# A decoder step on one core: two recurrences' small matrix products gathered into one group on the tensor engine

## The chip, the core and the metric

One core of one Trainium2 chip runs the whole step as one program. The metric is the device time of one launch in microseconds (us). Before the change it is 1133.66 us, the median of 3 runs (1133.45 to 1133.82).

## What is computed

One inference step of a hybrid decoder layer for 256 prompt tokens and 8 sample sequences of 8 tokens (320 tokens in all, model width 2048). One big projection of the normalised input feeds two recurrences; each is gated and projected, the two are merged by gates, and an output projection with a residual and a final norm ends the step. Cut to what matters here:

```python
h = rms_norm(x, norm_g)
p = jnp.einsum('nld,dp->nlp', h, w_in)            # 2048 -> 11,392 columns
# branch A (RWKV-7), 16 heads of 64, per token:
#   S_t = S_{t-1} diag(w_t) - (S_{t-1} kk_t)(kk_t * a_t)^T + v_t k_t^T ;  y_t = S_t r_t
y_a, s_a_new = rwkv7_recurrence(r_h, heads_a(decay), k_h, v_h, kk, heads_a(a), s_a)
# branch B (HGRN2), 8 heads, state 128 x 128, chunk by chunk:
#   S_t = diag(g_t) S_{t-1} + k_t v_t^T ;  o_t = S_t^T q_t
o_b, s_b_new = gla_chunkwise(heads_b(q_b), heads_b(k_b), heads_b(i_b), heads_b(log_g), s_b)
merged = sigmoid(p[gate_a]) * (y_a @ proj_a) + sigmoid(p[gate_b]) * (y_b @ proj_b)
y = x + merged @ w_out
```

All of it is float32; a large product is made of three passes in a rounded format (high*high, high*low, low*high), a small one is a plain float32 product, which the chip runs as two instructions.

## The kernel before

The program has three stages. A start normalises and transposes the input into two SBUF tiles, `hhi` and `hlo`. The **recurrence stage**, from about 30 to 696 us, is `record_all` (L1382): it goes over eight pairs `p` of A's heads, each with one head of B. For a pair it projects eight blocks of 128 columns (r, k, v, za for A; q, f, i, zb for B), each 16 x 3 products of 128x128 weights with 128x320 tokens into a PSUM tile named `mps`. I call these the *stream*: 3264 products, at L1441 in the profile. Then it computes `rwkv` (L780) and `hgrn` (L1163) for the pair. The last stage (from L1443 on) does the remaining gate columns, `proj_a`, `proj_b` and `w_out`; the change does not touch it.

In the recurrence stage nothing is issued as it is written. Every call goes to a `Recorder` (L69), which keeps a cost in ns for each operation, finds who depends on whom (`link`, L155) and then writes out an order for all engines together (`order`, L209). Each engine runs its own list in that order, so all its instructions stand at one line, L1441, the line that issues them. On the tensor engine the planner puts a small product into the list where it expects its operands to be there, 250 ns later than it computes (`MARGIN`), and fills the rest with stream products. So small products stand in the stream as *visits*: some stream products, one or more small ones, stream products again. The list is in order: if a small product's operand is late, the stream behind it waits too.

The tensor engine can also be cut into smaller tiles, for example four of 128 rows by 32 columns, whose products overlap. Products that are meant to run so are recorded as a *group* by `side_by_side` (L1360). The planner schedules the members of a group as if they all depended on whatever any of them depends on, and it accounts for each change of tile form. For B's operations it sets a wait of 6000 ns (`book.wait`, L1426 to L1428), by which B's group may be held back until another divided group opens the way.

The parts that the change touches, for one pair:

- *Pair products* of A (L895 to L907): for four chunks of 64 tokens and two heads, 64-row products as a group of eight into two PSUM tiles; for the samples (chunk 4) one 128x128 by 128x256 product, which holds both heads because `arp` is zero outside a head's own rows. Each result is masked into `g2`.
- *The turn of N* (L909 to L924): five transposes of `g2[:, ci, 0]`, for four chunks and the samples, copied into `xt` (ring `uB`) and from there into `M` (ring `uE`). The inverse of a triangular matrix is then built up from it in five doubling steps.
- *The chunk recurrence* `chunks` (L1013): per chunk the right side `rt`, which is `g2[:, ci, 0]` times `uv` plus, from the second chunk on, `arp` times the state, both added up in one PSUM tile; then two more products in a chain.
- *The samples' right side* in `samples` (L1054): a group of 12 products in four 128x32 tiles, into a tile of the ring `a` (three PSUM tiles for all of A).
- *B's group* (L1261): 42 products in 128x32 tiles. Behind it comes a transpose of `es` (L1279) and, ahead of it, one of `v` (L1181), both written for half the columns (profile form `128*64`).
- *The samples' decay* (L1086): GpSimd builds a diagonal tile `fd` twice in one buffer; each is read by one product.

The ring `y` is one more PSUM tile, used once a pair by the output products `py` (L1113).

## Time and profile before

| what | value |
|---|---|
| median of 3 runs | 1133.66 us |
| the profiled execution | 1133.88 us, its span 1132.1 us |
| TensorE (PE) busy | 1110.7 us, 98% of the span |
| VectorE (DVE) busy | 754.8 us, 67% |
| ScalarE (ACT) busy | 691.3 us, 61% |
| GpSimd (POOL) busy | 193.9 us, 17% |
| chain that ended last, by engine | PE 89%, DMA 3%, DVE 3%, issue 3% |

The profile is of one execution; a row gives an engine, a source line, an operation, the tiles it writes and reads, and the shapes. In the recurrence stage the line is always L1441, so operations are told apart by tiles and shapes. A tensor-engine row `128*32` is an instruction that uses 128 rows and 32 columns of the engine. A plain float32 product counts as two instructions. Tile `a` is any tile of A's PSUM ring, `b` one of B's, `y` the output ring; `uv`, `g`, `arp`, `bk`, `s0t`, `az`, `st`, `qz`, `es`, `fd` are as in the code; `pp` and `uB` belong to the doubling steps. In the timeline, instructions that follow each other with the same text stand in one row with their count, the start of the first, and the time until the last one's end; a PE row's length is modelled, so starts are what is measured.

### The profile page before, as it was taken

The numbers are of one execution on the slowest core, as the hardware profiler recorded it, in microseconds if no ns is written. First come the engines' busy times: TensorE is split into PE (matmuls) and PEld (weight loads), VectorE is DVE, ScalarE is ACT, GpSimd is POOL, SyncE is SP. The second block draws the span as 40 slices with busy tenths as digits, with TensorE's granted clock in tenths as the row PEclk, the third lists the DMA queues.
The fourth block names the chain that finished last, engine by engine and source line by source line (L and its number), as shares of the span: only waits on it lengthen the run. The fifth ranks groups of instructions, "written<-read, shape, count | busy, mean of one in ns | idle before, by whom it ended". The sixth has DMA issues, their size and how long they took to land.

```text
span 1132.1 us, 23282 instructions
## 1 busy us (share of the span) xinstructions
PE 1110.7 (98%) x9048; PEld 1072.6 (95%) x9048; DVE 754.8 (67%) x1586; ACT 691.3 (61%) x1580; POOL 193.9 (17%) x411
## 2 busy tenths in 40 slices
PE   6999999999999999999999999999999999999997
PEld 5998999999999999999999999999999999988886
DVE  7777788787887887878888776444444444436632
ACT  6767768777778678678677677444444444435322
POOL 9631131222321402302312200000000000000000
PEclk9999999999999999999999999999999999999999
DMA  5733645435435435445445345555555555587512
GB/s 177 198 112 97 169 115 134 139 108 138 131 112 155 132 98 152 130 114 148 117 114 153 112 125 146 150 151 149 154 150 150 150 149 149 149 252 250 186 38 93
DMA packets 283106, 159.85 MB, mean 141 GB/s; under 512 B 22893, under 2 KB 273264, under 8 KB 282356
## 3 DMA queue, kind: packets, MB, share of 16 engines
q1 hardware_dynamic: 282996, 158.37, 49.1%
q8 instruction: 71, 1.16, 0.4%
q14 instruction: 39, 0.32, 0.1%
HBM read 148.53 MB, written 9.81 MB: 140 GB/s over the span
## 4 chain that ended last, share of the span: by engine, by line
PE 89%; DMA 3%; DVE 3%; issue 3%; ACT 1%; POOL 1%; ACTq 0%; SPq 0%; POOLq 0%; DVEq 0%
PE mps L1441 40%; PE a L1441 11%; PE mps L360 6%; PE mps L361 6%; PE mps L359 6%; PE b L1441 3%; DMA raw<-in_w_out_dram 2%; PE po L1526 2%; PE po L1524 2%; PE po L1525 2%; PE ppb L360 2%; PE ppa L361 2%; PE ppa L360 2%; PE ppa L359 2%; PE ppb L359 2%
## 5 line engine op out<-in xcount | busy, mean ns | idle before, releaser
L1441 PE MATMUL mps<-hhi,wlo 128*128 128x320 f32 x1088 | 344.7, 317 | 0.0
L1441 PE MATMUL mps<-hhi,whi 128*128 128x320 f32 x1088 | 344.6, 317 | 0.0
L1441 PE MATMUL mps<-hlo,whi 128*128 128x320 f32 x1088 | 344.1, 316 | 0.0
L1441 PEld LDWEIGHTS mps<-hlo,whi 128*128 128x128 f32 x1088 | 204.9, 188 | 2.2 <-issue 1.2
L1441 PEld LDWEIGHTS mps<-hhi,whi 128*128 128x128 f32 x1088 | 204.8, 188 | 1.9 <-issue 0.8
L1441 PEld LDWEIGHTS mps<-hhi,wlo 128*128 128x128 f32 x1088 | 204.8, 188 | 1.4 <-issue 0.4
L349 ACT CAST whi<-raw 128x1024 fp32r<-128x1024 f32 x88 | 92.5, 1051 | 162.7 <-PE mps L360 107.3
L350 DVE TENSOR_TENSOR wlo<-raw,whi 128x1024 fp32r<-128x1024 f32 x88 | 107.9, 1226 | 125.0 <-ACT whi L349 124.8
L1441 DVE TENSOR_TENSOR wlo<-raw,whi 128x1024 fp32r<-128x1024 f32 x134 | 166.8, 1244 | 26.3 <-ACT whi L1441 24.5
L1441 ACT CAST whi<-raw 128x1024 fp32r<-128x1024 f32 x134 | 140.3, 1047 | 67.1 <-PE mps L1441 64.2
L359 PE MATMUL mps<-hhi,whi 128*128 128x320 f32 x448 | 138.4, 309 | 0.0
L360 PE MATMUL mps<-hlo,whi 128*128 128x320 f32 x448 | 138.4, 309 | 0.0
L361 PE MATMUL mps<-hhi,wlo 128*128 128x320 f32 x448 | 138.4, 309 | 0.0
L359 PEld LDWEIGHTS mps<-hhi,whi 128*128 128x128 f32 x448 | 84.1, 188 | 0.0
L360 PEld LDWEIGHTS mps<-hlo,whi 128*128 128x128 f32 x448 | 84.1, 188 | 0.0
L361 PEld LDWEIGHTS mps<-hhi,wlo 128*128 128x128 f32 x448 | 84.1, 188 | 0.0
L1513 DVE TENSOR_TENSOR wlo<-raw,whi 128x1024 fp32r<-128x1024 f32 x32 | 38.5, 1223 | 39.2 <-ACT whi L1512 36.4
L1512 ACT CAST whi<-raw 128x1024 fp32r<-128x1024 f32 x32 | 32.9, 1050 | 49.0 <-DMA raw<-in_w_out_dram 24.1
L1524 PE MATMUL po<-whi,mhi 128*128 128x512 f32 x128 | 50.1, 391 | 0.7 <-DVE gbt L1481 0.7
L1526 PE MATMUL po<-wlo,mhi 128*128 128x512 f32 x128 | 50.1, 392 | 0.1
L1525 PE MATMUL po<-whi,mlo 128*128 128x512 f32 x128 | 50.0, 391 | 0.0
L359 PE MATMUL ppa<-yah,whi 128*128 128x320 f32 x128 | 39.6, 309 | 0.0
(423 smaller groups left out, 2224.1 us busy)
## 6 DMA issues: line engine op xcount, KB each, us to landing
raw<-in_w_in_dram SPq DMA_DIRECT2D x194, 512.0 KB
raw<-in_w_out_dram SPq DMA_DIRECT2D x32, 512.0 KB
raw<-in_proj_a_dram SPq DMA_DIRECT2D x16, 512.0 KB
raw<-in_proj_b_dram SPq DMA_DIRECT2D x16, 512.0 KB
s<-in_state_hgrn_dram SPq DMA_DIRECT2D x8, 512.0 KB
out_dram<-s SPq DMA_DIRECT2D x8, 512.0 KB
s<-in_state_rwkv_dram SPq DMA_DIRECT2D x8, 256.0 KB
out_dram<-s SPq DMA_DIRECT2D x8, 256.0 KB
```

Of the source, the lines that this page charges most:

```text
L349: S.copy(hi[:, ks], raw[:, ks])
L350: sub.tensor_sub(lo[:, ks], raw[:, ks], hi[:, ks].bitcast(F32))
L359: T.matmul(dst, hi[:, q, :], xhi[:, k, :], start=(k == 0), stop=False)
L360: T.matmul(dst, hi[:, q, :], xlo[:, k, :], start=False, stop=False)
L361: T.matmul(dst, lo[:, q, :], xhi[:, k, :], start=False, stop=(k == nk - 1))
L1441: o.fn(*o.args, **o.kw)
L1512: S.copy(hi, raw)
L1513: V.tensor_sub(lo, raw, hi.bitcast(F32))
L1524: T.matmul(pt, h, hi, start=first, stop=False)
L1525: T.matmul(pt, l, hi, start=False, stop=False)
L1526: T.matmul(pt, h, lo, start=False, stop=end)
```

## The change

It makes one group of three sets of products. `rwkv` and `hgrn` become generators that hand out their products at a `yield`; `record_all` records both lists as one group and then runs the rest of each. The group has the samples' 12 products, 16 new 128x32 products which compute what `uv` gives to the right sides of all four chunks (they go into the ring `y`, are copied once into `rv`, and are added to the state's part by VectorE), and B's 42. `book.wait` is no longer set. The samples' pair products are made by head, in the group of the other pair products, and masked by two operations. For the turn of N, ScalarE first gathers two chunks in one tile `nd` (ring `big`), so three transposes do and one copy takes them out. The two half-width transposes of B take a full 128 columns.

```diff
         banks = [aps("pg") for _ in HS]
-        side_by_side([((banks[h][:, 128 * ci:128 * ci + 128], bk2[HS[h], ci]..., arp[HS[h], ci, :, h]), ...) for ci in range(4) for h in range(2)])
+        own = [ring(psy, "y", [128, 512], 1, F32, None), aps("pg")]
+        side_by_side([((banks[h][:, 128 * ci:128 * ci + 128] if ci < 4 else own[h][:, :128],
+                        bk2[HS[h], ci]..., arp[HS[h], ci, :, h]), ...) for ci in range(5) for h in range(2)])
...
-        ps = aps("pg")
-        T.matmul(ps[:, :256], bk2[:, 4]..., arp[:, 4]..., start=True, stop=True)
-        V.tensor_mul(g2[:, 4], ps[:, :256]..., mk[:, 2, :, None]...)
+        for h in range(2):
+            V.tensor_mul(g2[:, 4, :, h], own[h][:, :128]..., mk[:, 2])
+        nd = at("nd", (128, 2, 2, 64), tag="big")
+        for c_ in range(2):
+            S.copy(nd[HS[c_]], g2[HS[c_], c_:4:2, 0])
         ps = aps("pM")
-        for ci in range(5):
-            turn(ps, ci, g2[:, ci, 0].rearrange("p h t -> p (h t)"))
+        for cp in range(2):
+            T.transpose(ps[:, 128 * cp:128 * cp + 128], nd[:, cp].rearrange("p h t -> p (h t)"), ident)
+        T.transpose(ps[:, 256:384], g2[:, 4, 0].rearrange("p h t -> p (h t)"), ident)
-        S.copy(xt[:, 0:4]..., half(ps, 2))
-        S.copy(xt[:, 4], ps[:, 384:448])
+        S.copy(xt[:, 0:5].rearrange("p c t -> p (c t)"), ps[:, :320])
...
+        pr = ring(psy, "y", [128, 512], 1, F32, None)
+        psr = aps("psr")
+        work = []                       # first the samples' 12 products, as before
+        for ci in range(4):
+            for h in range(2):
+                for a_ in range(2):
+                    o_ = 64 * h + 32 * a_
+                    work.append(((pr[o_:o_ + 32, 64 * ci:64 * ci + 64], g2[:, ci, 0, h, 32 * a_:32 * a_ + 32],
+                                  uv[:, ci, h]), dict(start=True, stop=True)))
+        yield work
         def chunks():
-                ps = aps("pr")
-                T.matmul(ps[:, :128], g2[:, ci, 0]..., uv[:, ci]..., start=True, stop=st_ is None)
-                if st_ is not None:
-                    T.matmul(ps[:, :128], arp[:, ci, 0]..., st_, start=False, stop=True)
-                V.tensor_copy(rt[tk, 0], ps[HS[0], 0:64])
-                S.copy(rt[tk, 1], ps[HS[1], 64:128])
+                if st_ is None:
+                    V.tensor_copy(rt[tk, 0], pr[HS[0], 0:64])
+                    S.copy(rt[tk, 1], pr[HS[1], 0:64])
+                    rv = at("rv", (128, 3, 64), tag="uK")
+                    S.copy(rv.rearrange("p c v -> p (c v)"), pr[:, 64:256])
+                else:
+                    ps = aps("pr")
+                    T.matmul(ps[:, :128], arp[:, ci, 0]..., st_, start=True, stop=True)
+                    for h in range(2):
+                        V.tensor_add(rt[tk, h], ps[HS[h], 64 * h:64 * h + 64], rv[HS[h], ci - 1])
...
-        T.transpose(ps[0:64, 256:384], v[:, NP_:], ident)
+        T.transpose(ps[:, 256:384], v[:, NT - 128:], ident)
...
-        side_by_side([(x_, dict(start=True, stop=True)) for x_ in work])
+        yield [(x_, dict(start=True, stop=True)) for x_ in work]
...
-        T.transpose(ps[0:64, :128], es[:, 1], ident)
+        T.transpose(ps[:, :128], es.rearrange("p x t -> p (x t)"), ident)
...
-            rwkv(p, *(io[key] for key in ("r", "k", "v", "za")))
-            book.wait = book.WAIT
-            hgrn(p, *(io[key] for key in ("q", "f", "i", "zb")))
-            book.wait = 0
+            both = rwkv(p, ...), hgrn(p, ...)
+            side_by_side(next(both[0]) + next(both[1]))
+            for gen in both:
+                run(gen)
```

The planner then writes another order. Three places of it, all of TensorE; a product counts once here, and `mps` rows are the stream.

The third pair, before: first the samples' group (`s0t,az` and `uv,g`, 12 products), then, 60 stream products on, B's group of 42.

```order
L1441 MATMUL mps<-hhi,whi 128x320
L1441 MATMUL a_488<-s0t_497,az_500 32x64 x8
L1441 MATMUL a_488<-uv_495,g_0_502 32x64 x4
L1441 MATMUL mps<-hlo,whi 128x320
L1441 MATMUL a_486<-rhs_507,yz 128x128
```

```order
L1441 MATMUL mps<-hhi,whi 128x320
L1441 MATMUL b_524<-s_0_520,qz 32x128 x8
L1441 MATMUL b_523<-w_0_529,w_0_521 32x32 x8
L1441 MATMUL b_523<-w_0_528 32x32 x8
L1441 MATMUL b_523<-o_531 32x32 x8
L1441 MATMUL b_523<-ket_532 32x32 x4
L1441 MATMUL b_523<-ks_534,s_0_533 32x64 x4
L1441 MATMUL b_523<-w_0_529,w_0_521 32x32 x2
L1441 MATMUL mps<-hlo,whi 128x320
L1441 MATMUL a_486<-st_514,arp 128x128
```

The same pair in the changed kernel: one group of 70, then one stream product, then four small products that hang on it.

```order
L1448 MATMUL mps<-hhi,wlo 128x320
L1448 MATMUL a_488<-s0t_497,az_500 32x64 x8
L1448 MATMUL a_488<-uv_495,g_0_502 32x64 x4
L1448 MATMUL y_503<-uv_495,g_0_502 32x64 x16
L1448 MATMUL b_513<-s_0_509,qz 32x128 x8
L1448 MATMUL b_512<-w_0_518,w_0_510 32x32 x8
L1448 MATMUL b_512<-w_0_517 32x32 x8
L1448 MATMUL b_512<-o_520 32x32 x8
L1448 MATMUL b_512<-ket_521 32x32 x4
L1448 MATMUL b_512<-ks_523,s_0_522 32x64 x4
L1448 MATMUL b_512<-w_0_518,w_0_510 32x32 x2
L1448 MATMUL mps<-hhi,whi 128x320
```

What moved: the two groups stand at one place, with the 16 new products between them; the third pair's group comes after 1140 stream products, where the two came after 1117 and 1177. Over the stage, 22 visits held 128x32 products and 16 do now (8 of these are the output products); small products stand in 387 visits both times.

The first pair, the second `fd` product, before:

```order
L1441 MATMUL a_486<-fd_511,jr_sum 128x256
L1441 MATMUL mps<-hlo,whi 128x320
L1441 MATMUL mps<-hhi,wlo 128x320
L1441 MATMUL mps<-hhi,whi 128x320
L1441 MATMUL mps<-hlo,whi 128x320
L1441 MATMUL a_487<-rhs_507,yz 128x128
L1441 MATMUL a_488<-rhs_0_508,ys_503 128x128
L1441 MATMUL a_486<-fd_511,jr_sum 128x256
```

and now, with the first `fd` product right behind the group:

```order
L1448 MATMUL a_488<-fd_530,jr_sum 128x256
L1448 MATMUL a_486<-rhs_526,yz 128x128
L1448 MATMUL a_487<-rhs_0_527,ys_505 128x128
L1448 MATMUL b_513<-ident,es_524 128x128
L1448 MATMUL mps<-hhi,whi 128x320
L1448 MATMUL mps<-hlo,whi 128x320
L1448 MATMUL mps<-hhi,wlo 128x320
L1448 MATMUL mps<-hhi,whi 128x320
L1448 MATMUL a_486<-uv_495,bk_506 128x128
L1448 MATMUL mps<-hlo,whi 128x320
L1448 MATMUL a_488<-fd_530,jr_sum 128x256
```

What moved: between the two `fd` products stand five stream products and four small ones, where there were four and two; and `fd` now comes behind B's group, for which VectorE has by then made all operands. The second `fd` product stood after 353 stream products in this pair; the new group stands after 368.

## Rows read from the trace of the kernel before

**Rows 1.** The page's part 1: engine, busy us (share of the span) x instructions.

```profile
PE 1110.7 (98%) x9048; PEld 1072.6 (95%) x9048; DVE 754.8 (67%) x1586; ACT 691.3 (61%) x1580; POOL 193.9 (17%) x411
```

**Rows 2.** Busy time of each engine in a stretch of the recurrence stage: the stretch, its us, then PE, PEld, DVE, ACT, POOL busy (x instructions), granted clock, DMA share, GB/s.

```profile
200.00:280.00 80.00, 80.00 (x804) 77.86 (x793) 65.14 (x159) 56.90 (x151) 20.74 (x44) 1.00 0.46 126
```

**Rows 3.** A group of PE instructions by line, tiles and shape: xcount | busy us, mean ns of one | idle before.

```profile
L1441 PE MATMUL a<-uv,g 128*128 128x128 f32 x64 | 12.4, 275 | 0.0
```

**Rows 4.** PE's timeline, first pair, two stream products with 23 more between them (start us, us, what).

```profile
59.74 0.31 PE L1441 MATMUL mps<-hhi,wlo 128*128 128x320 f32 x1
...
63.26 0.31 PE L1441 MATMUL mps<-hhi,wlo 128*128 128x320 f32 x1
```

**Rows 5.** The same timeline: a visit of two float32 128x128 products (four instructions), and one of the same with the chunk's `uv,g` product behind them; in each, one stream product that isn't shown stands ahead of the last row.

```profile
85.18 0.31 PE L1441 MATMUL mps<-hhi,wlo 128*128 128x320 f32 x1
85.33 0.60 PE L1441 MATMUL a<-pp,uB 128*128 128x128 f32 x4
...
85.92 0.31 PE L1441 MATMUL mps<-hlo,whi 128*128 128x320 f32 x1
...
90.25 0.31 PE L1441 MATMUL mps<-hhi,whi 128*128 128x320 f32 x1
90.40 0.60 PE L1441 MATMUL a<-pp,uB 128*128 128x128 f32 x4
90.84 0.39 PE L1441 MATMUL a<-uv,g 128*128 128x128 f32 x2
...
91.21 0.31 PE L1441 MATMUL mps<-hhi,wlo 128*128 128x320 f32 x1
```

**Rows 6.** PE's timeline, third pair: the samples' group alone.

```profile
253.83 0.31 PE L1441 MATMUL mps<-hhi,whi 128*128 128x320 f32 x1
254.06 0.43 PE L1441 MATMUL a<-s0t,az 128*32 128x64 f32 x16
254.31 0.29 PE L1441 MATMUL a<-uv,g 128*32 128x64 f32 x8
254.54 0.41 PE L1441 MATMUL mps<-hlo,whi 128*128 128x320 f32 x1
```

**Rows 7.** PE's timeline, third pair: B's group alone (its other products lie between the second row and the third), then a visit and the transpose of `es`; one stream product that isn't shown stands ahead of the last row.

```profile
267.31 0.31 PE L1441 MATMUL mps<-hhi,whi 128*128 128x320 f32 x1
267.55 0.64 PE L1441 MATMUL b<-s,qz 128*32 128x128 f32 x16
...
268.76 0.42 PE L1441 MATMUL mps<-hlo,whi 128*128 128x320 f32 x1
269.02 0.38 PE L1441 MATMUL a<-st,arp 128*128 128x128 f32 x2
269.16 0.40 PE L1441 MATMUL mps<-hhi,wlo 128*128 128x320 f32 x1
269.39 0.28 PE L1441 MATMUL b<-ident,es 128*64 128x128 f32 x1
...
269.66 0.31 PE L1441 MATMUL mps<-hlo,whi 128*128 128x320 f32 x1
```

**Rows 8.** PE's timeline, fourth pair: both groups in one visit.

```profile
338.28 0.31 PE L1441 MATMUL mps<-hhi,whi 128*128 128x320 f32 x1
338.52 0.43 PE L1441 MATMUL a<-s0t,az 128*32 128x64 f32 x16
...
338.88 0.62 PE L1441 MATMUL b<-s,qz 128*32 128x128 f32 x16
...
340.07 0.41 PE L1441 MATMUL mps<-hlo,whi 128*128 128x320 f32 x1
```

**Rows 9.** PE's timeline, third pair: the pair products' group, the samples' product behind it, and the turn's transposes.

```profile
226.25 1.16 PE L1441 MATMUL a<-arp,bk 64*128 64x128 f32 x16
227.34 0.41 PE L1441 MATMUL mps<-hhi,wlo 128*128 128x320 f32 x1
227.59 0.59 PE L1441 MATMUL a<-arp,bk 128*128 128x256 f32 x2
227.83 0.50 PE L1441 MATMUL mps<-hhi,whi 128*128 128x320 f32 x1
228.17 0.31 PE L1441 MATMUL mps<-hlo,whi 128*128 128x320 f32 x1
...
229.05 0.71 PE L1441 MATMUL a<-ident,g 128*128 128x128 f32 x5
```

**Rows 10.** The first pair around 95 us: PE's, POOL's and DVE's timelines (idle time before an instruction and who ended it in brackets), then the group of all `fd` operations: xcount, ns min/median/max, first and last start.

```profile
97.25 0.39 PE L1441 MATMUL a<-fd,jr_sum 128*128 128x256 f32 x1 [1.68 <-POOL fd L1441]
...
94.63 2.57 POOL L1441 TENSOR_TENSOR fd<-id,fq 128x256 fp32r<-128x256 f32 x1 [22.01 <-PE a L1441]
...
94.77 1.21 DVE L1441 TENSOR_TENSOR wlo<-raw,whi 128x1024 fp32r<-128x1024 f32 x1
...
96.51 0.21 DVE L1441 TENSOR_TENSOR qz<-es,q 128x64 f32<-128x64 f32 x1
...
L1441 POOL TENSOR_TENSOR fd<-id,fq x16: 607/616/2572, 51.7 to 660.3; 128x256 fp32r<-128x256 f32 x16
```

**Rows 11.** Groups of DVE instructions, as in rows 3.

```profile
L1441 DVE COPY rhs<-a 64x64 f32<-64x64 f32 x40 | 8.6, 215 | 8.5 <-PE a L1441 3.8 <-ACT rhs L1441 3.8
L1441 DVE TENSOR_TENSOR g<-a,mk 128x256 f32<-128x256 f32 x8 | 3.3, 417 | 0.0
```

More of the change, by code (lines that the diff above doesn't have):

```diff
@@ L895, in rwkv @@
         banks = [aps("pg") for _ in HS]
-        side_by_side([((banks[h][:, 128 * ci:128 * ci + 128], bk2[HS[h], ci].rearrange("p j t -> p (j t)"),
-                        arp[HS[h], ci, :, h]), dict(start=True, stop=True)) for ci in range(4) for h in range(2)])
+        own = [ring(psy, "y", [128, 512], 1, F32, None), aps("pg")]
+        side_by_side([((banks[h][:, 128 * ci:128 * ci + 128] if ci < 4 else own[h][:, :128],
+                        bk2[HS[h], ci].rearrange("p j t -> p (j t)"), arp[HS[h], ci, :, h]),
+                       dict(start=True, stop=True)) for ci in range(5) for h in range(2)])
         for h in range(2):
@@ L1011, in rwkv @@
         states = []
+        pr = ring(psy, "y", [128, 512], 1, F32, None)
+        psr = aps("psr")
+        work = []
+        for step in range(3):
+            for h in range(2):
+                for a_ in range(2):
+                    l_, r_ = (az[:, h, a_, 32 * step:32 * step + 32], s0t[:, 2 * a_ + step, 64 * h:64 * h + 64]) \
+                        if step < 2 else (g2[:, 4, 0, h, 32 * a_:32 * a_ + 32], uv[:, 4, h])
+                    o_ = 64 * h + 32 * a_
+                    work.append(((psr[o_:o_ + 32, :64], l_, r_), dict(start=step == 0, stop=step == 2)))
+        for ci in range(4):
+            for h in range(2):
+                for a_ in range(2):
+                    o_ = 64 * h + 32 * a_
+                    work.append(((pr[o_:o_ + 32, 64 * ci:64 * ci + 64], g2[:, ci, 0, h, 32 * a_:32 * a_ + 32],
+                                  uv[:, ci, h]), dict(start=True, stop=True)))
+        yield work
         def chunks():
@@ L1017, in chunks @@
                 tk = HS[c_]
[L1018 to L1021 removed]
                 rt = at("rhs", (128, 2, 64))
[L1023 to L1024 removed]
+                if st_ is None:
[5 more added lines that the diff above has]
+                    ps = aps("pr")
+                    T.matmul(ps[:, :128], arp[:, ci, 0].rearrange("p h t -> p (h t)"), st_, start=True, stop=True)
+                    for h in range(2):
+                        V.tensor_add(rt[tk, h], ps[HS[h], 64 * h:64 * h + 64], rv[HS[h], ci - 1])
                 yield
@@ L1054, in samples @@
         def samples():
-            ps = aps("psr")
-            work = []
-            for step in range(3):
-                for h in range(2):
-                    for a_ in range(2):
-                        l_, r_ = (az[:, h, a_, 32 * step:32 * step + 32], s0t[:, 2 * a_ + step, 64 * h:64 * h + 64]) \
-                            if step < 2 else (g2[:, 4, 0, h, 32 * a_:32 * a_ + 32], uv[:, 4, h])
-                        o_ = 64 * h + 32 * a_
-                        work.append(((ps[o_:o_ + 32, :64], l_, r_), dict(start=step == 0, stop=step == 2)))
-            side_by_side(work)
             rhs = at("rhs2", (128, 2, 64))
-            V.tensor_copy(rhs[0:64, 0], ps[HS[0], :64])
-            S.copy(rhs[0:64, 1], ps[HS[1], :64])
+            V.tensor_copy(rhs[0:64, 0], psr[HS[0], :64])
+            S.copy(rhs[0:64, 1], psr[HS[1], :64])
             yield
@@ L1283, in hgrn @@
             for j in (0, 2):
-                S.copy(k3[32 * j:32 * j + 32, g], ps[own, :128])
-            V.tensor_sub(k3[32:64, g], ps[own, :128], k3[0:32, g].bitcast(F32))
+                S.copy(k3[32 * j:32 * j + 32, g], ps[64 + 32 * g:96 + 32 * g, :128])
+            V.tensor_sub(k3[32:64, g], ps[64 + 32 * g:96 + 32 * g, :128], k3[0:32, g].bitcast(F32))
         ps = bps("pot")
```

15 lines of the change are left out of this document (3 added, 12 removed).

## The prediction

> **What bounds the kernel now.** I read the page's busy shares first, then the stretches, then TensorE's timeline. TensorE is busy for 98% of the span, VectorE for 67% [rows 1]. In a stretch of the recurrence stage TensorE is busy for all of 80.00 us at the full granted clock, VectorE for 65.14, ScalarE for 56.90 [rows 2]. So in this stage the time is the length of TensorE's list, and each thing has to be priced by what it takes out of that list, not by its own length: products overlap, and a row's 0.31 us of a stream product is not its share. The timeline gives the share. From the start of one stream product to that of the 24th behind it pass 63.26 - 59.74 = 3.52 us, 0.1467 us each [rows 4]. The price of a visit is then the time between the stream products around it, less 0.147 for each stream product in it.
>
> The cover that hides other engines is the stream itself: while a chain of small operations waits for VectorE or ScalarE, stream products run. It has 3264 products in both orders, and in both the last output products stand some 100 of them (15 us at 0.147) ahead of the stream's end, so the stage's end is not moved by a longer chain.
>
> **Part by part**, per pair of heads, then times eight.
>
> *Right sides' value part, out.* A visit with four instructions of 128x128 takes 85.92 - 85.18 - 2 x 0.147 = 0.45 us; with the chunk's `uv,g` product behind them 91.21 - 90.25 - 2 x 0.147 = 0.67 [rows 5]. So one such product (two instructions) costs 0.22 us. There are 64 instructions [rows 3], 32 products: **-7.0 us**.
>
> *The same part, in 128x32 tiles.* It is 16 products, 32 instructions of 128x32 with 64 columns, the very shape of the `s0t,az` and `uv,g` rows. In the fourth pair 24 of these start between 338.52 and 338.88 us, 0.015 us each [rows 8]; 32 take 0.48 us, **+3.8 us** in all. Bounds: B's 84 instructions take 268.76 - 267.55 = 1.21 us, 0.0144 each [rows 7], 3.7 us in all; the last eight of a group with the way out of it take 254.54 - 254.31 = 0.23, 0.029 each [rows 6], 7.4 in all. I take 0.015, since it is read inside such a group, where the new ones stand.
>
> The Trainium skill speaks against this price: the page "TensorE: Matmul & The Clock Gate", section "Wait — 56ns, not 53.3ns?", says that starts of small matmuls are never less than about 25 ns apart. By that the term would be 32 x 25 ns = 0.8 us a pair, 6.4 us in all. The trace disagrees, with 15 ns.
>
> *Samples' pair products.* The visit of the 128x256 product takes 228.17 - 227.34 = 0.83 us; without it the two steps would be 0.25 (what follows any group: 227.59 - 227.34) and 0.147, so 0.43 goes. Four instructions are added to a group in which 16 take 227.34 - 226.25 = 1.09 us, 0.068 each [rows 9]: +0.27. Together -0.16, **-1.3 us**.
>
> *Turn of N.* Five transposes take 0.71 us from the first start to the last end, and one lasts about 0.28 [rows 7, 9]: (0.71 - 0.28) / 4 = 0.11 each. Two go: **-1.8 us**. The two copies into `nd` come before the transposes on the chain, but the stream covers a chain; ScalarE pays for them, beside the bound.
>
> *One group for two.* Alone, the samples' group takes 254.54 - 253.83 - 0.147 = 0.56 us [rows 6], B's 268.76 - 267.31 - 0.147 = 1.30 [rows 7]; both in one visit take 340.07 - 338.28 - 0.147 = 1.64 [rows 8]. That saves 0.22, and one slow step behind a group (269.02 - 268.76 = 0.26 in place of 0.147) [rows 7], 0.33 in all. In two pairs they already stood together, so six gain: -2.0. But in four of these six B's group had the samples' 64x64 group (`pds`) beside it, which now stands alone in all eight. That gives back between nothing and 4 x 0.33; I take the middle, +0.7. Net **-1.3 us**.
>
> *Half-width transposes.* The `es` visit takes 269.66 - 269.16 - 2 x 0.147 = 0.21 us [rows 7], a full-width transpose 0.11. If each of 16 lost that 0.10, it would be 1.6; the one of `v` I have no clean row for. Between 0 and -1.6 I take **-0.4 us**, since such a transpose is a change of tile form only where it stands alone.
>
> *Waits.* In the first pair TensorE stood still for 1.68 us for the second `fd`: GpSimd took 2.57 us for what takes 0.616 in the median, while VectorE ran operations with two SBUF operands, a 1.21 us weight subtraction among them [rows 10]. In the new order the two `fd` products are further apart, and VectorE's products for B are done ahead of the group. So I expect this wait to go: -1.7. New small ones will come, since four products stand one stream product behind the group and hang on copies out of it: I put +0.7. Net **-1.0 us**, between -1.7 and nothing.
>
> *Costs beside the bound.* VectorE gets six additions for three copies at 0.215 us, 0.65 us a pair, and one mask operation of 0.417 us becomes two, under 0.42 more [rows 11]. On 65.14 us in 80 [rows 2] that is 83% at most. What hides it is TensorE's list; if that cover were gone, it would be 8 x 1.07 = 8.6 us. No DMA is added or removed.
>
> The sum: -7.0 + 3.8 - 1.3 - 1.8 - 1.3 - 0.4 - 1.0 = -9.0 us. The profiled execution took 1133.88 us, 0.22 above the median, so the median goes from 1133.66 to **1124.7 us**.
>
> **Rivals.**
>
> *New waits eat half.* The visit behind the group needs `rt` and both halves of `rhs`, copied by VectorE and ScalarE out of a group that ends 0.147 us earlier. A copy is 0.215 us [rows 11], and a weight cast of ScalarE's can stand in front of it. At 0.5 us a pair this is +4: 1128.7 us. For it: the list is in order, and one late operand did hold it for 1.68 us [rows 10]. Against: the samples' and the values' products come first in the group, and B's 84 instructions, 1.2 us [rows 7], run behind them while the copies are made. Chance 0.14.
>
> *B's operands come late, and it gets slower.* The samples' side has to wait for B's last operand now, and a late one holds TensorE, stream included. In the first pair B's last operand, `qz`, was made at 96.51 us, behind a weight subtraction of 1.21 us [rows 10]. If every group waited as long as the `fd` of the first pair, 1.68 us, it would be 13.4 us on -8.0 (the sum without waits): 1139 us. It decides from 1.0 us a pair. Against: that was ahead of the second `fd` product at 97.25 us [rows 10], which stood after 353 stream products; the new group comes after 368, 2.2 us of stream later, and the planner adds 250 ns for every operand. Chance 0.04.
>
> *Starts 25 ns apart.* If the new products did not run as closely as those in the rows, but at 25 ns, the group would be 32 x 0.010 = 0.32 us a pair longer, +2.6: 1127.3 us. Rows 6 and 8 speak against it; for it only that the group gets longer, 140 instructions, than any in the rows. Chance 0.04. It is the rule of "TensorE: Matmul & The Clock Gate" cited above.
>
> *TensorE is not what is short.* If VectorE or ScalarE sets the pace somewhere in a pair, a shorter list makes TensorE wait for weights, and 1133 us stays. For it: VectorE is 81% busy and gets more. Against: TensorE is busy for 80.00 of 80.00 us [rows 2]. Chance 0.06. The Trainium skill warns of this in "TensorEngine Tiling (Array Packing)", section "PSUM Bottleneck": tiling makes TensorE faster but not the copies out of PSUM.
>
> **How the numbers follow.** The forecast has 0.72. A difference of 0.2%, 2.3 us, is about what a measurement of this kernel can tell from none. Forecast, eaten half and 25 ns are all faster by more: 0.72 + 0.14 + 0.04 = 0.90; within 0.2%: 0.06; slower: 0.04. The range: with the low ends (values' part -0.1, `pds` -0.7, half-width -1.2, waits -0.7) it is 2.7 below, 1122.0; with the high ends (+3.6, +0.6, +0.4, +1.0) 5.6 above, 1130.3, which takes in the first and third rival. The prices are read from starts given to 0.01 us, so I round outward below, and give 1121.5 to 1130.0.
>
> **What would show it.** Right: the group's visit with 140 instructions takes about 2.1 us (1.64 + 0.48); `uv,g` in 128*128 form is gone, and its chunk visits hold a lone `st,arp`; the pair products' group takes 0.27 longer with no 128x256 visit behind it; TensorE's only long wait for POOL is gone; the last stage takes as long as before. Wrong: PE idle time in front of `rhs,yz` or of the group's first product, with ACT or DVE as releaser; a stream step above 0.147 away from visits; or a group longer than 2.5 us.

## The result and the profile of the changed kernel

The changed kernel takes 1124.47 us (median of 6 runs, 1123.9 to 1124.7); the kernel before, beside it on the same chip, 1133.74. The ratio is 0.9917, 95% interval 0.9904 to 0.9929. The forecast was 1124.7 with a range of 1121.5 to 1130.0. The profiled execution took 1124.7 us with a span of 1122.0.

Page, part 1, and the stretch from 200 to 280 us (length, then PE, PEld, DVE, ACT and POOL busy with counts, granted clock, DMA share, GB/s). They answer to [rows 1, 2]:

```profile
PE 1102.9 (98%) x9240; PEld 1066.5 (95%) x9240; DVE 760.4 (68%) x1618; ACT 693.2 (62%) x1572; POOL 192.8 (17%) x411
...
200.00:280.00 80.00, 79.66 (x792) 77.61 (x791) 66.30 (x165) 59.90 (x157) 18.27 (x42) 1.00 0.45 125
```

TensorE has 192 instructions more and is busy for 7.8 us less. It is still what is short, but not for the whole stretch: 0.34 us are idle in it now, and we come to them. VectorE and ScalarE do a little more beside the bound; VectorE 5.6 us in all, where 8.6 was priced.

TensorE's timeline in the third pair, from the last stream product ahead of the joint group to the end of the visit behind it (start, duration, line, output<-inputs, tile, shape, count). It answers to [rows 6 to 8]:

```profile
252.47 0.31 PE L1448 MATMUL mps<-hhi,wlo 128*128 128x320 f32 x1
252.71 0.43 PE L1448 MATMUL a<-s0t,az 128*32 128x64 f32 x16
252.95 0.29 PE L1448 MATMUL a<-uv,g 128*32 128x64 f32 x8
253.07 0.63 PE L1448 MATMUL y<-uv,g 128*32 128x64 f32 x32
253.51 0.62 PE L1448 MATMUL b<-s,qz 128*32 128x128 f32 x16
...
254.70 0.42 PE L1448 MATMUL mps<-hhi,whi 128*128 128x320 f32 x1
254.96 0.28 PE L1448 MATMUL a<-fd,jr_sum 128*128 128x256 f32 x1
255.08 0.38 PE L1448 MATMUL a<-rhs,yz 128*128 128x128 f32 x2
255.30 0.39 PE L1448 MATMUL a<-rhs,ys 128*128 128x128 f32 x2
255.52 0.27 PE L1448 MATMUL b<-ident,es 128*128 128x128 f32 x1
255.55 0.39 PE L1448 MATMUL mps<-hlo,whi 128*128 128x320 f32 x1
...
258.76 0.31 PE L1448 MATMUL mps<-hhi,wlo 128*128 128x320 f32 x1
259.00 0.66 PE L1448 MATMUL a<-big,rhs 64*64 64x256 f32 x8
259.60 0.41 PE L1448 MATMUL mps<-hhi,whi 128*128 128x320 f32 x1
```

Start the reading at the stream rows. The group of 140 instructions stands between 252.47 and 254.70: 2.23 us, less 0.147 for the stream product, 2.09 (2.088 before rounding). Its new piece, the 32 instructions `y<-uv,g`, runs from 253.07 to 253.51, 0.014 us each. Behind it the visit with `rhs` shows no idle time in brackets: the copies out of the group are in time. The group `a<-big,rhs` (`pds`) stands alone.

The pair products of the fourth pair, which answer to [rows 9] (there it is the third pair); the 128x256 visit behind them is gone:

```profile
301.25 1.16 PE L1448 MATMUL a<-arp,bk 64*128 64x128 f32 x16
...
302.57 0.42 PE L1448 MATMUL mps<-hlo,whi 128*128 128x320 f32 x1
302.82 0.31 PE L1448 MATMUL mps<-hhi,wlo 128*128 128x320 f32 x1
...
305.67 0.40 PE L1448 MATMUL mps<-hlo,whi 128*128 128x320 f32 x1
305.90 0.27 PE L1448 MATMUL a<-ident,bks 128*128 128x128 f32 x1
305.93 0.39 PE L1448 MATMUL mps<-hhi,wlo 128*128 128x320 f32 x1
306.16 0.31 PE L1448 MATMUL mps<-hhi,whi 128*128 128x320 f32 x1
```

The group takes 302.57 - 301.25 = 1.32 us from its first start, against 1.09 before: 0.23 for four instructions. The last four rows are a transpose of full width that stands alone: 306.16 - 305.67 - 2 x 0.147 = 0.20 us. We need it for the half-width ones.

TensorE's waits (operation, line, releaser, total us, times, longest) and GpSimd's `fd` (min/median/max ns), which answer to [rows 10]:

```profile
PE a L1448 <- DVE pp L1448: 0.7, 2, 0.3
...
L1448 POOL TENSOR_TENSOR fd<-id,fq x16: 607/614/1651, 51.0 to 648.2; 128x256 fp32r<-128x256 f32 x16
```

The 1.68 us for `fd` are gone, though one `fd` still takes 1.65 us instead of 0.61: nobody waits for it now. A new pair of waits stands there, for `pp`. One of the two, on three engines:

```profile
231.39 1.13 DVE L1448 TENSOR_TENSOR uB<-id,uB 128x160 f32<-128x160 f32 x1
232.44 0.48 DVE L1448 TENSOR_TENSOR pp<-a,lvz 128x320 f32<-128x320 f32 x1
...
231.30 1.04 POOL L1448 TENSOR_TENSOR big<-bk,seq 128x512 f32<-128x512 f32 x1
...
232.41 0.31 PE L1448 MATMUL mps<-hhi,wlo 128*128 128x320 f32 x1
233.07 0.85 PE L1448 MATMUL a<-pp,uB 128*128 128x128 f32 x6 [0.34 <-DVE pp L1448]
```

`uB` takes 1.13 us on VectorE while GpSimd works on `big`; `pp` stands behind it, and TensorE starts `pp,uB` 0.66 us behind the stream product before it. The bracket's 0.34 is only the time with nothing left in the engine: what a visit lost is the distance of the starts, 0.58 us by the visit's price.

### A price list to read the experiments by

To compare the kernels I fitted one price for each kind of instruction, visit and group to all visits of the kernel before, and applied these prices to the order of each other kernel (*list*, us over the recurrence stage, an estimate). *Visits* is what the trace has, that is, the time between stream products beyond 0.147 each. The last column is the part of the difference in visits over 0.12 us above their price, with their number. List and visits come from one execution of each kernel.

| kernel | median us | list | visits | over 0.12 |
|---|---|---|---|---|
| before | 1133.74 | 181.7 | 188.3 | 5.6 in 13 |
| changed | 1124.47 | 173.2 | 178.9 | 3.9 in 10 |
| vals_full | 1126.61 | 176.7 | 181.9 | 4.0 in 10 |
| pair_whole | 1124.66 | 175.1 | 178.9 | 2.6 in 7 |
| turn_five | 1125.40 | 174.9 | 179.9 | 3.7 in 11 |
| two_groups | 1123.56 | 174.7 | 178.5 | 2.7 in 5 |
| half_width | 1123.85 | 173.3 | 177.8 | 3.1 in 11 |
| vals_twice | 1133.34 | 176.9 | 188.5 | 10.1 in 13 |
| vals_twice_apart | 1130.39 | 178.6 | 183.3 | 2.2 in 7 |
| margin_0 | 1131.36 | 173.2 | 185.5 | 9.8 in 35 |
| margin_400 | 1121.61 | 173.2 | 175.4 | 1.1 in 4 |
| two_margin_400 | 1121.51 | 174.1 | 175.7 | 0.7 in 2 |

So the list became 8.5 us shorter and the rest 0.9: 6.6 before, 5.7 now. That is the 9.5 us by which the stage is shorter. The four parts undone one by one add 3.5, 1.9, 1.7 and 1.5 to the list, 8.6 in all: the list is the sum of its parts. The times are not, and the experiments are about that.

Three things limit the table. The medians' intervals reach some 1.4 us to either side, so a difference of about one us between two of these kernels is not told by the medians. The stage's first visit, at 37 us, waits for `ast`, and this wait is shorter where the stream starts later: in half_width, margin_0 and the two kernels with `400` it starts at 30.1 us in place of 29.0 to 29.3, and their visits are up to 1.0 us lower for that alone. And vals_twice_apart has a stop of 0.7 us away from any visit, which the column leaves out.

### The profile page after: what moved, and what is told of

It is laid out like the page before. It is cut to its first block, busy times and chain, and to the rows that moved or that the text cites. A ratio compares the mean times of both kernels' runs of the same rounds, so it can differ in the third digit from the quotient of the medians.

```text
span 1122.0 us, 23659 instructions
## 1 busy us (share of the span) xinstructions
PE 1102.9 (98%) x9240; PEld 1066.5 (95%) x9240; DVE 760.4 (68%) x1618; ACT 693.2 (62%) x1572; POOL 192.8 (17%) x411
## 4 chain that ended last, share of the span: by engine, by line
PE 94%; POOL 2%; ACT 2%; issue 1%; DVE 0%; DMA 0%; ACTq 0%; POOLq 0%; DVEq 0%
PE mps L1448 41%; PE a L1448 10%; PE mps L359 6%; PE mps L360 6%; PE mps L361 6%; PE b L1448 3%; PE po L1531 3%; PE po L1533 3%; PE po L1532 3%; PE ppa L359 2%; PE ppb L360 2%; PE ppb L359 2%; PE ppa L360 2%; PE ppb L361 2%; PE ppa L361 2%; PE y L1448 1%
## 5 line engine op out<-in xcount | busy, mean ns | idle before, releaser
L1448 POOL TENSOR_TENSOR vm<-v,seq 96x512 fp32r<-96x512 f32 x16 | 16.9, 1054 | 200.1 <-ACT uK L1448 152.4
```

What stands on the lines that cost most here:

```text
L1448: o.fn(*o.args, **o.kw)
```

## Experiments

All times are medians, the kernel before beside them 1133.74 to 1133.93. The theory (L) is the prediction's: the time is the length of TensorE's list, read in prices per visit, plus a few waits. Its rivals change from run to run.

### The values' part as 128x128 products again

```
-        for ci in range(4):
...
-                    work.append(((pr[o_:o_ + 32, 64 * ci:64 * ci + 64], g2[:, ci, 0, h, 32 * a_:32 * a_ + 32],
-                                  uv[:, ci, h]), dict(start=True, stop=True)))
...
+                T.matmul(ps[:, :128], g2[:, ci, 0].rearrange("p h t -> p (h t)"), uv[:, ci].rearrange("p h v -> p (h v)"), start=True, stop=st_ is None)
```

> The change with one part undone: the values' part of the right sides is again one 128x128 product a chunk, added up with the state's part in PSUM; the 16 products of 128x32 leave the group (54 products stay in it), and the copy rv and the additions go. Theory L (time is the length of TensorE's list): +7.0 us for 32 products at 0.22, -3.8 for 32 x 8 instructions at 0.015, so 3.2 slower than the changed kernel, 1127.7 us, and the group's visit shrinks from 2.09 to about 1.6 us. Rival C (small products in a group cost 25 ns a start): only 0.6 slower, 1125.1. Rival W (the gain came from waits that the new order lost): within 1 us of the changed kernel, and PE's waits of the old profile come back.

Measured: 1126.61 (1126.55 to 1127.59), ratio 0.9936 [0.9923, 0.9948], 2.1 above the changed kernel. The median lies between L and C; the stage decides. In the profiled execution its visits are 3.0 us longer, near the 3.2 that L adds and far from the 0.6 of C. (The whole is 2.9 longer, 1127.59 against 1124.7, but in that execution TensorE also waits 0.7 us for a weight behind the stage.) The list by the fitted prices is 3.5 longer. W's waits of the old profile do not come back. The joint group of the third pair:

```profile
254.21 0.31 PE L1437 MATMUL mps<-hhi,wlo 128*128 128x320 f32 x1
...
256.00 0.41 PE L1437 MATMUL mps<-hhi,whi 128*128 128x320 f32 x1
```

It takes 256.00 - 254.21 - 0.147 = 1.64 us, as in seven of the eight pairs. So the 32 instructions are worth 2.09 - 1.64 = 0.45 us in the group, 0.014 each.

### The samples' pair products as one 128x256 product again

```
+        T.matmul(ps[:, :256], bk2[:, 4].rearrange("p j t -> p (j t)"), arp[:, 4].rearrange("p x h t -> p (x h t)"),
+                 start=True, stop=True)
+        V.tensor_mul(g2[:, 4], ps[:, :256].rearrange("p (x h t) -> p x h t", x=2, h=2),
+                     mk[:, 2, :, None].to_broadcast([128, 2, 2, 64]))
```

> The change with the samples' pair products as one 128x256 product again, in a visit of its own or behind the group, masked by one operation. Theory L: +0.16 us a pair as first priced, +1.3 us, and up to +1.9 by the rows of all eight pairs: 1125.8 to 1126.4 us. Rival Y (the ring y, which the by-head product shares with the output products, makes the group wait): undoing it gains, 1124.0 or less.

Measured: 1124.66 (1124.46 to 1125.05), 0.9917 [0.9903, 0.9931]: 0.2 above. The list is 1.9 longer, which is 0.24 a pair and above the 0.16 predicted; but the two waits for `pp` are not there, and the visits add up to the same 178.9 us. Neither side is right by the time: the gain is there in the list and paid back in waits. Two of these, gaps of 0.6 and 0.3 us between instructions, are stops of the kind that the last section explains.

### Five transposes again in the turn of N

```
+        for ci in range(5):
+            turn(ps, ci, g2[:, ci, 0].rearrange("p h t -> p (h t)"))
```

> The change with the turn of N undone: five transposes of the masked products again, no gathering copies nd, two copies out. Theory L: two transposes more a pair at 0.11 us, +1.8 us, about 1126.3 us. Rival N (the chain counts: the two gathering copies, about 0.3 to 0.4 us each on ScalarE, stand ahead of the transposes on the chain of the doubling steps): undoing it gains 0.5 us or more, 1124.0 or less.

Measured: 1125.40 (1125.21 to 1125.81), 0.9924 [0.9911, 0.9938]: 0.9 above, between the two. The list has the 1.7 us. In its profiled execution one joint group stands still for 0.9 us, with no releaser, and there is a second gap, of 0.5 us, at 413.8 us; the last section explains both. Without them the time would hardly have moved, so the turn's gain in time stays unsettled between 0 and 0.9 us.

### The two groups apart again

```
-            side_by_side(next(both[0]) + next(both[1]))
-            for gen in both:
-                run(gen)
+            side_by_side(next(both[0]))
+            run(both[0])
+            book.wait = book.WAIT
+            side_by_side(next(both[1]))
+            run(both[1])
+            book.wait = 0
```

> The change with the merging alone undone: the samples' and values' products are one group, B's 42 another, and B's wait of 6000 ns is set again; all other parts stay. Theory L: the new list has 23 visits with 128x32 groups where the changed kernel has 16; the separate visits cost 0.33 us each where both are alone, part of it given back where B's group finds the samples' 64x64 group: +1.3, between 0.7 and 2.3, so about 1125.8 us. Rival W (one group makes TensorE wait for the later branch, and apart is better): 1124.5 or less.

Measured: 1123.56 (1123.35 to 1125.49), 0.9911 [0.9897, 0.9924]: 0.9 *below* the changed kernel. L expected 1.3 above and fails here: undoing the merge costs nothing. That it is a gain of 0.9 is within the noise. TensorE's timeline in the third pair:

```profile
249.23 0.31 PE L1451 MATMUL mps<-hlo,whi 128*128 128x320 f32 x1
...
250.39 0.41 PE L1451 MATMUL mps<-hhi,wlo 128*128 128x320 f32 x1
...
255.21 0.31 PE L1451 MATMUL mps<-hhi,wlo 128*128 128x320 f32 x1
255.35 0.38 PE L1451 MATMUL a<-st,arp 128*128 128x128 f32 x2
255.66 0.66 PE L1451 MATMUL a<-big,rhs 64*64 64x256 f32 x8
256.26 0.65 PE L1451 MATMUL b<-s,qz 128*32 128x128 f32 x16
...
257.47 0.41 PE L1451 MATMUL mps<-hhi,whi 128*128 128x320 f32 x1
```

The samples' group alone takes 250.39 - 249.23 - 0.147 = 1.01 us. B's group shares its visit with `big,rhs`, as it does in seven of eight pairs here (in the eighth the planner put the two groups together all the same): 2.11 with a `st,arp` product of 0.22 in it, 1.89. Together 2.90. Merged it is 2.09 and, for the `big,rhs` group that is left alone, 259.60 - 258.76 - 0.147 = 0.69: 2.78. So in this plan the merge saves 0.12 a pair, some 0.9 in seven pairs, and late visits take it back: they are 3.9 us with the merge and 2.7 without. That the merge itself makes them late is not shown.

### Half-width transposes

```
-        T.transpose(ps[:, :128], es.rearrange("p x t -> p (x t)"), ident)
+        T.transpose(ps[0:64, :128], es[:, 1], ident)
```

> The changed kernel with the two transposes of B, of v and of es, for half the columns again (form 128*64). Theory L: up to 0.10 us for each of 16 where the change of tile form costs, as first priced +0.4 us (0 to 1.6): about 1124.9 us, and the visit with es takes 0.88 us where it takes 0.78. Rival 0 (the form costs nothing beside other products): 1124.5 us and 0.78.

Measured: 1123.85 (1123.72 to 1124.48), 0.9911 [0.9898, 0.9925]. The visit with `es`:

```profile
254.91 0.41 PE L1448 MATMUL mps<-hhi,whi 128*128 128x320 f32 x1
...
255.72 0.27 PE L1448 MATMUL b<-ident,es 128*64 128x128 f32 x1
255.74 0.39 PE L1448 MATMUL mps<-hlo,whi 128*128 128x320 f32 x1
```

From 254.91 to 255.74 are 0.83 us; with the whole tile it is 255.55 - 254.70 = 0.85. The same products stand in both visits, so the change of form costs nothing there: rival 0. The transpose of `v` was not read by itself; the time gives it no room for a gain.

### The values' products twice, in the group and apart

Two kernels compute the sixteen values' products a second time, into unused columns. In the first they are in the same group:

```
-        for ci in range(4):
+        for ci in range(8):
             for h in range(2):
                 for a_ in range(2):
                     o_ = 64 * h + 32 * a_
-                    work.append(((pr[o_:o_ + 32, 64 * ci:64 * ci + 64], g2[:, ci, 0, h, 32 * a_:32 * a_ + 32],
-                                  uv[:, ci, h]), dict(start=True, stop=True)))
+                    work.append(((pr[o_:o_ + 32, 64 * ci:64 * ci + 64], g2[:, ci % 4, 0, h, 32 * a_:32 * a_ + 32],
+                                  uv[:, ci % 4, h]), dict(start=True, stop=True)))
```

> The changed kernel with the 16 values' products made twice in the group (the second time into unused columns of the same PSUM tile): 86 products in the group instead of 70. It prices 32 instructions of 128x32 inside the group by themselves. Theory L (0.015 us a start, time is TensorE's list): the group's visit grows from 2.09 to about 2.55 us, +3.8 us in all, about 1128.3 us. Rival C (25 ns a start): visit 2.9 us, +6.4, 1130.9 us. Rival T (the price at a group's end, 0.029): +7.4, 1131.9 us. Rival F (they fit into time that TensorE loses anyway): under +1 us.

Measured: 1133.34 (1132.8 to 1134.9), 0.9998 [0.9989, 1.0007], 8.9 above the changed kernel. The group's price is L's exactly, in four of eight pairs: 2.53 us, 0.45 more for 32 instructions, 0.014 each. In the other four it is 3.9 to 4.2. The third pair, and TensorE's waits:

```profile
253.51 0.30 PE L1448 MATMUL mps<-hhi,wlo 128*128 128x320 f32 x1
253.75 0.43 PE L1448 MATMUL a<-s0t,az 128*32 128x64 f32 x16
...
255.70 0.21 PE L1448 MATMUL b<-w 128*32 128x32 f32 x2
257.32 0.30 PE L1448 MATMUL b<-o 128*32 128x32 f32 x12 [1.40 <-issue]
...
257.80 0.41 PE L1448 MATMUL mps<-hhi,whi 128*128 128x320 f32 x1
```

```profile
PE b L1448 <- issue: 5.6, 4, 1.5
```

TensorE stops in the middle of the group, between two of B's products, and the releaser is "issue": no semaphore that the trace knows held it (the last section finds what did). The four stops make 6.4 of the 10.1 us in the table (the four groups are 1.4 to 1.7 us longer than the other four). They are no price of the work, as the second kernel shows, which has the same instructions in shorter pieces.

In it the loop gives the second sixteen to a list of their own (`more`), which is recorded as a group ahead of the joint one and stands some 150 stream products ahead of it:

```
+        yield more
         yield work
...
+            side_by_side(next(both[0]))
             side_by_side(next(both[0]) + next(both[1]))
```

> The change, with the sixteen values' products computed twice again, but the second set in a group of its own, which stands some 150 stream products ahead of the joint group (the output is the reference's). The instructions are the same as with both sets in one group; the longest dense piece is 140 instructions again in place of 172. With one long group, four of eight groups stopped inside for 1.4 to 1.7 us with no releaser. Theory B (the stop belongs to the long dense piece): no stop inside any group, the joint group 2.09 us as in the change, and the price is that of the extra group alone: 32 x 0.014 and about 0.22 for a visit of its own form, 0.67 us a pair, 5.3 in all: 1129.8 us. Rival W (the stop comes from the amount of instructions, wherever they stand): stops of over 1 us stay, in some other place, and the time is as with one long group or more, 1133 to 1135 us. Decided by the waits inside groups that end in issue, first, and by the time: under 1131 B, over 1132.5 W.

Measured: 1130.39 (1129.09 to 1131.01), 0.9968 [0.9956, 0.9981]. The joint group in the third pair:

```profile
254.04 0.31 PE L1452 MATMUL mps<-hhi,wlo 128*128 128x320 f32 x1
254.28 0.43 PE L1452 MATMUL a<-s0t,az 128*32 128x64 f32 x16
...
256.28 0.41 PE L1452 MATMUL mps<-hhi,whi 128*128 128x320 f32 x1
```

No group stops, only one wait with the releaser "issue" is left (0.5 us, in front of a stream product), the joint group takes 256.28 - 254.04 - 0.147 = 2.09 us, and the kernel is 3 us faster than with one long group, although its list is 1.7 longer. B holds: with the products in shorter pieces no group stops here. The wait that is left is of the same kind, as the last section shows.

### The kernel before with the second `fd` in another buffer

```
-                fd = at("fd", (128, NSEQ, 32), dt=F32R)
+                fd = at("fd", (128, NSEQ, 32), dt=F32R) if hf == 0 else yh[:, :256].rearrange("p (s k) -> p s k", k=32)
```

> The kernel before with one thing taken away: the second fd tile has its own buffer (the one of yh, free at that time), so GpSimd need not wait for the first fd product and the first pair's wait of 1.68 us has no cause. The planner moves other groups for it: the same prices of visits give a list that is 2.5 us longer. Theory L (list plus waits): +2.5 - 1.7, about 1134.5 us, with no wait of TensorE for fd. Rival W (that wait cost nothing, other work filled it): +2.5, 1136.2 us. Rival R (a planner's list cannot be priced by visits): below 1133.0.

Measured: 1135.16 (1132.85 to 1137.02), 1.0008 [0.9999, 1.0017]. TensorE's longest wait in the stage is no longer for `fd`:

```profile
PE y L1441 <- issue: 2.3, 1, 2.3
```

The wait went and a stop of 2.3 us inside a long piece (B's group and the output group in one visit, at 503 us) came. So the wait can be taken away by itself, but this run doesn't show the 1.7 us in the time, and between L and W it does not decide.

### The masked tile `big` on ScalarE

```
-            G.tensor_mul(bm, bk[:, 4, None].to_broadcast([128, 4, 128]), seq4[:, :, None].to_broadcast([128, 4, 128]))
+            for si in range(4):
+                S.activation(bm[:, si], bk[:, 4], AF.Copy, scale=seq4[:, si:si + 1])
```

> The changed kernel with the samples' masked tile (big<-bk,seq, 1.04 us on GpSimd) made by four ScalarE operations instead. In the changed kernel's trace the third and the fifth pair lose 0.58 us each in front of a pp,uB product, where VectorE's uB operation with two SBUF operands took 1.13 us beside that GpSimd operation, and 0.7 where it ran alone. Theory P (these two engines slow each other): both waits go, 1.2 us less, about 1123.3 us; the list is as long by prices. Rival S (ScalarE gets about 1.2 us more a pair, 10 in all, and becomes late): new waits for ACT, 1125 us or more. Rival 0: the waits come from a plan that is too tight anyway and stay: 1124.5.

Measured: 1124.41 (1123.66 to 1124.84), 0.9914 [0.9901, 0.9928]. Both waits of 0.58 us for `pp` are gone, as expected, and with `big` off GpSimd all eight `uB` take 0.32 to 0.42 us, where the two longest beside it took 1.12 and 1.13: GpSimd's operation is what slowed `uB`. But other waits came: some 0.4 us each in front of `pp,uB` in the second and the fourth pair, a stop of 1.1 us inside the first pair's group, and 0.8 us that the view puts down to `attc`:

```profile
PE b L1449 <- issue: 1.1, 1, 1.1
...
PE a L1449 <- DVE attc L1449: 0.8, 1, 0.8
```

P is right on the place and wrong on the time. The last section shows that the `attc` row is a stop as well; without the two stops, some 2 us, this execution would be under the 1123.3 us that P expected (an estimate from the two gaps, 1.2 and 1.0 us).

### The planner's allowance

The planner puts a product outside the stream 250 ns behind the planned end of its operand. Two kernels change only that number.

```
-    APART, MARGIN, WAIT, OVER = 10, 250, 6000, 130
+    APART, MARGIN, WAIT, OVER = 10, 0, 6000, 130
```

> The change, with the planner's allowance for an operand of a product outside the stream at 0 in place of 250 ns (MARGIN). The list's price is the same to 0.1 us, since visits and groups are nearly the same. Theory M (the waits left in the change are products planned too close behind their operand): the two 0.58 us waits of the masked product, and others, grow or multiply: 387 visits in 8 pairs, and if one in ten now comes 0.25 us early it is 10 us; I expect 2 to 10 us more, 1126.5 to 1134.5. Rival 0 (the allowance is not what they hang on; the late ones are late by a disturbed engine, by more than 250 ns): within 1.0 us of 1124.5.

Measured: 1131.36 (1130.85 to 1132.53), 0.9981 [0.9972, 0.9990], 6.9 above. The list is the same; 35 visits are late by over 0.12 us instead of 10. One of them is a stop of 1.3 us with the releaser "issue", right behind a joint group; the other 34 make 8.3 of the 9.8 us. In nearly all of them a product or its weights start 0.03 to 0.07 us behind the VectorE, ScalarE or GpSimd operation that makes the operand: they are late operands.

```
-    APART, MARGIN, WAIT, OVER = 10, 250, 6000, 130
+    APART, MARGIN, WAIT, OVER = 10, 400, 6000, 130
```

> The change, with the planner's allowance at 400 ns in place of 250. The list's price is the same to 0.1 us. Theory M: what is late by under 0.15 us goes, and the two waits of 0.58 shrink to some 0.43: of 3.9 us of waits over 0.12 about 1 to 2 go, 1122.5 to 1123.5 us. Rival 0: the pieces move, other products meet other disturbances, 1124.5 within 1.0 us. A gain of under 1 us can't be told from none by its time; the waits in front of the masked product tell then.

Measured: 1121.61 (1121.36 to 1122.68), 0.9895 [0.9880, 0.9911], 2.9 *below* the changed kernel. Late visits: 4. The visit of `pp` in the third pair:

```profile
235.06 0.31 PE L1448 MATMUL mps<-hlo,whi 128*128 128x320 f32 x1
235.21 0.78 PE L1448 MATMUL a<-pp,uB 128*128 128x128 f32 x6
235.79 0.39 PE L1448 MATMUL mps<-hhi,wlo 128*128 128x320 f32 x1
```

It has no wait. But here `uB` takes 0.33 us, since the new plan does not put it beside `big`, so this place is not the allowance's alone. Of the changed kernel's 3.9 us of late visits, 1.1 are the stage's first visit, 1.2 the two waits for `pp`, and some 1.6 seven late ones of at most 0.5 us, which is what M speaks of and the size that it gave. All of these are gone; a wait for `pp` of 0.3 and a stop of 0.5 came. The stage ends 2.5 us earlier (683.4 against 685.9 us). Theory M holds on both sides; that the step down is 2.9 us and not 1 to 2 is in part the new plan's luck.

### A version that beats both

The kernel of the two groups, with an allowance of 400 ns.

> The candidate: the change with the two recurrences' products as two groups again, each with its own wait (1123.56 us by itself), and the allowance at 400 ns. Its list is 0.6 us cheaper by the unit prices than with 250, and its waits over 0.12 were 2.7 us. Theory M: some 1 us of these go too, 1122.0 us. Rival 0: 1123.5 within 0.7 us. Faster than the change by the time in either case, by 0.9 to 2.5 us.

Measured: 1121.51 (1121.38 to 1121.76), 0.9892 [0.9879, 0.9906]. It is 3.0 us faster than the changed kernel, and no faster than margin_400 alone (0.1 us). It does not compare one group with two: in four of the eight pairs the planner put the two groups together again, as one piece of 140 instructions (visits at 252, 334, 411 and 646 us).

## Why the prediction was right

The predicted -9.0 us came as -9.2 in the profiled execution, and the likeliest case was the one that came. The mechanism holds: the time is the length of TensorE's list plus a few waits, and the list without waits, forecast at -8.0, came as -8.5. That the total is nearer than most of its terms is luck. By its steps:

- **Values' 128x128 products out (-7.0) and 128x32 tiles in (+3.8).** Right. The tiles cost 0.014 us each in the group (predicted 0.015), 3.6 us in all, measured three times: in the changed kernel, in vals_full and in vals_twice. Undone, the list is 3.5 us longer and the time 2.1. A floor of 25 ns between starts, the rule of the Trainium skill, "TensorE: Matmul & The Clock Gate", section "Wait — 56ns, not 53.3ns?", does not show: 32 starts take 0.44 us and not 0.8.
- **Samples' pair products (-1.3).** Right in sign, a little small: the four instructions cost 0.23 us and not 0.27, and undone the list has 1.9. In time it is 0.2, since the list without it happens to have no late `pp`, and has two stops instead.
- **Turn of N (-1.8).** In the list 1.7. In time between 0 and 0.9.
- **One group for two (-1.3).** Undone in two_groups, the list has 1.5 by the fitted prices, 0.9 by rows, and the time has nothing. Against the kernel before, the group visits, `pds` with them and the values' 0.45 us taken off, are some 1.3 us shorter over the eight pairs, which is the forecast; there `pds` did stand beside B's group in four of six pairs. But apart, in the changed kernel's plan, it stands there in seven, and the merge is worth less. What the term left out is the plan behind a later, larger group: the late visits differ by 1.2 us between the two kernels, as much as the term.
- **Half-width transposes (-0.4).** Wrong: nothing. The step that failed is the comparison: I set the 0.21 of a lone half-width transpose [rows 7] against the 0.11 of one in a row of five. A lone one of full width takes 0.20: the difference was that of standing alone, not of the form.
- **Waits (-1.0).** Right in sum, -0.9, and in its first part: the 1.68 us for `fd` went. The new ones were put in the wrong place: not behind the group, but in front of `pp,uB` (2 x 0.58), a chunk's `st,arp` with `vm,k` (0.4 to 0.5 by the fitted prices) and two `rhs,yz` (0.26 each).
- **What it did not have.** The stream starts 0.2 us earlier (29.0 against 29.3 us), what follows the stage takes 0.4 us less, and the profiled execution has 2.7 us outside the span against 1.8. With the stage's 9.5 us that makes the 9.2; the three nearly cancel.

Of the rivals, none came. New waits did not eat half; B's operands are never late for the group; TensorE remains what is short. But the size of the second-order effect was missed: how the pieces fall into the plan is worth 7 us up and 3 down, by one number of the planner; the 3 alone is more than any part of the change but the first.

## What to carry to other kernels

Where one engine's list is the bound, price each edit by the distance of the stream's starts around it, from rows of the same form: that gave a sum good to 0.5 us. Then look at how late operands are, for single edits under some 2 us drown in that: here a plan with 150 ns more allowance for operands was 2.9 us faster, while the merge of the groups, the turn and the pair products, 5.1 us of list, moved the time by -0.9, +0.9 and +0.2 us when undone. And don't make a dense group as long as it can be: one of 172 short instructions stopped in four of its eight places, waiting for its own instructions.

## What the runs showed that I had not expected

TensorE stopped inside a group of 172 short instructions in four of eight pairs, for 1.4 to 1.7 us, at a different product each time; once each for 0.9 and 1.2 us in groups of 140 (turn_five, after_bm_act); never in the eight groups of the changed kernel's profile. The DMA rows of the trace give a hint. In vals_twice the instruction queue moves one packet while a stopped group runs (253.7 to 255.7 us), and no packet begins in the stop (255.7 to 257.4):

```profile
q8 instruction: 1, 0.02, 3.6%
...
DMA packets 0, 0.00 MB, mean 0 GB/s; under 512 B 0, under 2 KB 0, under 8 KB 0
```

Over the whole execution it is

```profile
q8 instruction: 74, 1.21, 0.4%
```

74 packets of 16 KB, and TensorE's rows in the trace, products, weight loads and a few of its sequencer, are 19,134, which is 74.7 x 256; in the changed kernel they are 18,624, 72.8 x 256, and 73 packets. So a packet goes with 256 of TensorE's instructions. Number the rows and the packets from nought, and the stops are no longer at different places: all twelve waits of the stage with the releaser "issue", in eight kernels, stand in front of row 449 + 256 n (a product, or twice its weight load), where n is the packet's number, and so do the `attc` row of after_bm_act and a gap of 0.3 us in pair_whole. In each, row 449 + 256 n starts 2.2 to 2.8 us after packet n began. Of 982 packets in fourteen traces, none has that row earlier than 2.2 us after its own start.

So the stops are waits for instructions. No run moves the packets by themselves, but no other reading puts fourteen stops on one row in 256. It also says why length counts: in a group the rows pass at two in 0.014 us, in the stream at two in 0.147, so a packet that begins early in a long group has its row come too soon. The changed kernel's packet at 1.06 us into a group of 140 (410.99 us) does no harm, since its row comes 3.7 us later, behind the group; the nearest miss in its profile is 2.7 us.

VectorE's `uB` took 1.13 us beside GpSimd's `big`, which started 0.09 us ahead of it, and 0.33 in margin_400, where `big` did not run beside it; with `big` on ScalarE (after_bm_act) no `uB` takes more than 0.42. (The 0.72 of pair_whole, which I had taken for one alone, stood 0.53 us beside `big`.) So it is the operation on GpSimd that holds up `uB`, and a product that is planned by the usual duration is late then. GpSimd's `fd` took 1.65 us in place of 0.61; what holds it up was not tried by itself.
